# Splitting the output weights during the row maxima, and loading operands of pair 2 earlier, in a streaming encoder step

## The chip, the cores and the metric

The kernel runs on one core of a Trainium2 chip. The metric is the device time of one execution in microseconds (us); the figure of a kernel is the median of its runs. TensorE (PE) multiplies, with its weight loads shown as PEld; VectorE (DVE), ScalarE (ACT) and GpSimd (POOL) work on tiles in SBUF and PSUM; SyncE (SP) issues the transfers. Each engine takes its instructions in the order in which they were put into its queue, and waits on the first that is not ready.

## The reference

One layer of a streaming encoder is computed for a prompt of 2048 rows and a sample (decode) of 64 rows, with 1024 columns. One projection gives the input of an S5 branch, its gate, q, k, v, the gate of the attention, and forget logits. The attention has 8 heads of 64 columns, with a bias from the running sum of the forget logits:

```
logf = log_sigmoid(f_logit + b_f);  cum = cumsum(logf)
s = q k^T * scale + cum_q - cum_k, masked to pos_k <= pos_q
y_att = (softmax(s) v) * silu(z_a)
mixed = concatenate([y_ssm, y_att])            # (2048 + 64) x 1024
y = x + gate * (mixed @ w_out)                 # w_out is 1024 x 1024
```

The decode rows also attend to a cache of 512 rows. All data are float32; besides y, the kernel returns k, v, logf and the S5 states.

## The kernel before, in words

**Number format.** A float32 product is made as three products of two parts: `split` writes hi, rounded, on ACT (L319), and lo = x - hi on DVE (L323) or, where no engine is named, on POOL through `padd` (L205).

**Stages.** The input projection ends at about 620 us of the span, the S5 gate at about 800, attention (`Attn.run`) at about 1217, the output projection (`Out.run`) at 1391.

**Attention** goes over 20 tiles of a pair of heads and up to 512 query rows. A tile is done in units of two blocks of keys: TensorE makes scores into a `twin` of two PSUM banks, ACT exponentiates them into `p` (L354), DVE or POOL sums `p` into `acc` (L1489) for the denominators, and TensorE multiplies `p` with `vt` into `bank`. At a tile's end the sums are turned into a logarithm and an exponential `w` (two L354 on ACT), and `z`, the gated output, is multiplied on DVE (L1504) and POOL (L205) and stored in `ma_d` (L1519). Between the blocks the loop works ahead for later tiles: `step` loads k and q, `turn` transposes them on TensorE and splits them, and `maxima` makes each query row's largest score: TensorE computes the scores a first time and DVE adds the bias `cb` and takes the maximum (`pb`, `pm`, L1411). Three lists say what is still open: `todo` and `loaded` (k and q to be loaded, to be transposed), `mx` (maxima to be made), `smq` (maxima to be transposed into `sm`).

**Weights.** `Out.weights` is a generator which `Attn.run` advances twice per unit once all lists are empty. It loads the 16 blocks of w_out, 128 x 512 each, into a ring `ost` of three places (L1749, on SP), and two loads later splits a block: `ohb` on ACT, `olb` on POOL. Then it takes memory for the operands of the output, loads pair 0 of the S5 half (`load`, L1827), loads and splits the decode rows (L1909, L1910), and fetches the prepared operands t1 to t4 from DRAM (L1720). What is left of it `Out.run` finishes.

**Output.** The mixed rows are taken as pairs p = 0 to 7 of 128-row tiles. Pair 0 is multiplied plainly (`plain`: i the row tile, n the column half, j the half of the inner dimension; 0 is S5, 1 is attention). Pairs 1 to 7 use seven products instead of eight (`product`): sums and differences s1 to s4 of a pair's quarters a11, a12, a21, a22 are made by `differ` (1 and 3 on POOL, 2 and 4 on DVE: L1838, L1842) and split by ACT and DVE. The raw quarters come by `load(p)`: one 512 KB transfer from `ms_d` (tag m0) and one from `ma_d` (tag m1), each tag with one place. Evictions of PSUM into the `ot` ring of six are on DVE (L1878, L1881, L1882, L1816) and ACT (L1875); `residual` loads x (L1807), POOL adds (L205), SP stores the rows (L1821). `Out.run` is written as a fixed order: within it, each engine takes its instructions as the program has them, while in attention a scheduler places them.

Of the kernel before, what the change touches and what calls it, by code (L numbers as in the profile page):

```python
# [9 lines left out]
F32R = mybir.dt.float32r  # L10
# [7 lines left out]
P = 128  # L18
# [1164 lines left out]
class Attn:  # L1183
# [322 lines left out]
    def sums(self, tile):  # L1506
# [11 lines left out]
        e.pmul(tile.z, w[:, :n].rearrange("p (c t) -> p t c", t=TC), tile.z)  # L1518
        e.nc.sync.dma_start(e.ma_d[P * tile.hp:P * tile.hp + P, :, 64 * tile.qt:64 * tile.qt + n // TC], tile.z)  # L1519

    def run(self, out):

        e = self.e
# [2 lines left out]
            self.mem.ring(tag, int(1024 * kb), n)  # L1526
        self.hold("cb", 4, 3)
        weights = out.weights()
        pend = done = None
        self.forced = 0  # L1530
        self.vload(0)
        for i, (hp, qt) in enumerate(self.order):
# [15 lines left out]
            for u in range(0, len(blocks), PVG):  # L1548
                self.step()
                group = []  # L1550
                for kd, t in blocks[u:u + PVG]:
                    group.append(self.scores(tile, kd, t))
                    self.maxima()
                free = True
                if done and u:
                    self.sums(done)
                    done = None
                    free = False
                if pend:
                    self.mix(*pend)  # L1560
                    if pend[3]:
                        done = pend[0]
                pend = tile, group, u == 0, u + PVG >= len(blocks)
                if not u:
                    self.vload(i + 1)
                if free:
                    self.turn()
                if not (self.todo or self.loaded or self.mx or self.smq):
                    if not self.given:
                        out.mem.add(self.ring("kn"))  # L1570
                    out.mem.add(self.spare("cb", "ks", "qs", "sm"))
                    next(weights, None)
                    next(weights, None)
            if tile.acc[1] is not None and not tile.end:
# [2 lines left out]
        if done:  # L1577
            self.sums(done)

        out.mem.add(self.spare("vt"))  # L1580
        self.cur = self.seen = len(self.order)
        out.mem.add(self.spare("cb", "ks", "qs", "sm"))
        out.mem.join()
        for _ in range(16):
            if not out.cast:
# [82 lines left out]
class Out:  # L1668
# [12 lines left out]
    def __init__(self, e):  # L1681
        self.e = e
        self.mem = Region(e.nc)
        self.pre = Region(e.nc, R_PRE)
        self.b, self.a, self.x, self.acc, self.tmp, self.gate = {}, {}, {}, {}, {}, {}
        self.d, self.raw = [], []
        self.near = self.cast = False
        self.ops = {}

    def raw_operands(self, i):  # L1690
# [31 lines left out]
    def weights(self):  # L1722


        e = self.e
        mem = self.mem
        blocks = [(i, j) for i in range(2) for j in range(2)]

        def wait(n):
            while mem.room(2048) < n:  # L1730
                yield

        yield from wait(5)
        mem.ring("ost", 2048, 3)
        late = []

        def part():
            st, key = late.pop(0)
            h, l = (mem.tile([P, 512], F32R, name="o%s%s%d" % ((x,) + key)) for x in "hl")
            e.split(st, h, l, keep=True)  # L1740
            self.b[key] = h, l

        for k in range(4):
            for i, j in blocks:
                yield from wait(2)
                if len(late) == 2:
                    part()
                st = mem.tile([P, 512], F32, name="ost")
                e.nc.sync.dma_start(st, self.block(i, j, k))  # L1749
# [2 lines left out]
        while late:  # L1752
            yield from wait(2)
            part()
            yield
        for x in "hl":
            for name, n in (("a11", 1), ("a12", 1), ("a22", 2), ("s4", 1)):
                yield from wait(n)
                mem.ring("m" + x + name, 2048, n)
            mem.rings["m%sa21" % x] = mem.rings["m%ss4" % x]  # L1760
        while mem.room(4096) < 2:
            yield
        for j in range(2):
            mem.ring("m%d" % j, 4096, 1)
        self.load(0, 0)
        for j in range(2):
            yield from wait(2)
            mem.ring("ms%d" % (j + 1), 2048, 1)
# [1 line left out]
            self.decode_load(j)  # L1770
            yield
        yield
        for name in ("a11", "a21"):
            self.split(0, name, keep=True)
            yield
        for j in range(2):
            self.decode_split(j)
            yield
        self.cast = True
        for s in (1, 0):  # L1780
            for n in (1, 0):
                if s == n == 0:
# [152 lines left out]
    def run(self, weights):  # L1935

        e = self.e
        for tag, kb, n in (("x", 4, 1), ("ot", 2, 6), ("ms4", 2, 1), ("mhs2", 2, 1), ("mls2", 2, 1), ("mhs3", 2, 1),
                           ("mls3", 2, 1)):
            self.mem.ring(tag, 1024 * kb, n)  # L1940
        for i in range(2):
            m = self.a[0, "a%d2" % (i + 1)] = self.temp().rearrange("p (k c) -> p k c", k=4)
            e.nc.sync.dma_start(m, e.ma_d[:, 0, P * i:P * i + P].rearrange("(k p) c -> p k c", p=P))
        self.load(1, 1)
        for _ in weights:
            pass
        self.residual(2)
        self.decode(1)
        self.decode(0)

        self.fetch("t3", 3, [self.mem.at("late", x, [P, 512], F32R) for x in self.mem.rings["ost"][2][1:]])
        for i, n in ((0, 1), (1, 1), (0, 0), (1, 0)):
            self.plain(i, n, 0)
        for k in range(4):
# [2 lines left out]
        self.split(0, "a12", "a22")  # L1957
        self.differ(1, 1)
        self.differ(1, 3)
        self.differ(1, 2)  # L1960
        self.differ(1, 4)
        self.split(1, "a11", "s2")
        self.plain(0, 1, 1)
        self.plain(0, 0, 1)
        self.split(1, "s1", "a12")
        self.plain(1, 1, 1)
        self.split(1, "s3", "a22")
        self.load(2)
        self.plain(1, 0, 1)
        for p in range(1, 8):  # L1970
            q = p + 1 if p < 7 else 0
            self.split(p, "s4")
# [179 lines left out]
```

## Time and profile before

| | |
|---|---|
| runs | 1387.33, 1392.0, 1394.06 us, median 1392.0 |
| profiled execution | 1393.23 us, of which the span is 1391.4 us, mean granted clock 0.981 |
| PE, PEld busy | 1312.5 us (94%), 1031.9 us (74%) |
| DVE busy | 968.5 us (70%) |
| ACT busy | 652.0 us (47%) |
| POOL busy | 520.5 us (37%) |
| DMA | 204.92 MB, 147 GB/s on average |

The span runs from the first to the last instruction; 1.83 us of the execution lie around it. Busy shares are averages over stages with different limits: in the projections and the output TensorE is nearly always busy, so that any gap on it there is lost time, whereas other engines' gaps are not. A row of the timeline gives the start, the duration, the engine, the line, what is written and read, and in square brackets how long the engine had been idle before, and what ended that. A row of the waits gives the engine and line that waited, what it waited for, the total in us, how often, and the longest.

### The profile page before, as it was taken

To read this page: it belongs to the slowest core of one execution; us is meant where nothing else is said; L and a number is where in the kernel's file an instruction comes from. 1 tells how busy PE (TensorE), PEld (TensorE's weight loads), DVE (VectorE), ACT (ScalarE), POOL (GpSimd) and SP (SyncE) were. 2 spreads that over 40 slices of the span, in tenths; PEclk is the share of its full clock that TensorE was granted. 3 is DMA by queue.
4 is the path that set the end of the run, shared out by engine and by line. 5 is a ranking of instruction groups with operands and counts; after the bars stand their busy time and mean duration, and the time that the engine had idled before them with its cause. 6 is when DMAs were issued, how large, how long until landed. Compare 5 with 4: busy or idle time off the path is not lost.

```text
span 1391.4 us, 25886 instructions
## 1 busy us (share of the span) xinstructions
PE 1312.5 (94%) x9164; PEld 1031.9 (74%) x9164; DVE 968.5 (70%) x2404; ACT 652.0 (47%) x1710; POOL 520.5 (37%) x502
## 2 busy tenths in 40 slices
PE   5888999999999899999999899999999989898998
PEld 2886999998889899998879755555555554387887
DVE  3635896977877679864218877786787885446775
ACT  3645356567453576573315335445445445522211
POOL 1100254556534354452004113423423426743453
PEclk9899999999999999999999889999999999999999
DMA  9885333543546836446249624134121133495552
GB/s 342 318 309 124 100 86 94 154 123 107 163 133 217 282 110 180 145 141 196 84 138 291 202 73 121 32 91 125 43 70 48 40 65 79 146 330 169 182 164 78
DMA packets 249476, 204.92 MB, mean 147 GB/s; under 512 B 91296, under 2 KB 217340, under 8 KB 248322
## 3 DMA queue, kind: packets, MB, share of 16 engines
q1 hardware_dynamic: 249346, 203.27, 47.6%
q8 instruction: 72, 1.18, 0.4%
q14 instruction: 58, 0.48, 0.1%
HBM read 137.68 MB, written 65.53 MB: 146 GB/s over the span
## 4 chain that ended last, share of the span: by engine, by line
PE 63%; DVE 11%; DMA 6%; POOL 4%; issue 4%; ACT 3%; SPq 1%; DVEq 0%; ACTq 0%; POOLq 0%
PE low L154 25%; PE twin L154 13%; PE bank L154 12%; PE last L154 7%; PE glu L154 3%; DVE pb L1411 2%; PE bank L157 2%; DMA wst<-in_w_in_dram 1%; POOL qss L329 1%; POOL olb L205 1%; DMA lt<-t 1%; DVE acc L1489 1%; ACT p L354 1%; DVE ev L650 1%; DVE wlo L323 1%
## 5 line engine op out<-in xcount | busy, mean ns | idle before, releaser
L154 PE MATMUL low<-whi,h 128*128 128x256 f32 (+1 forms) x1584 | 296.3, 285 | 6.5 <-DVE th L609 3.5
L154 PE MATMUL low<-h,whi 128*128 128x256 f32 (+2 forms) x1152 | 277.6, 332 | 0.4 <-DVE h L323 0.3
L154 PEld LDWEIGHTS low<-whi,h 128*128 128x128 f32 x1584 | 247.9, 189 | 10.0 <-DVE th L609 3.7
L1411 DVE CUSTOM_DVE_ANT_0 pb<-twin,cb 128x512 bf16<-128x512 f32 (+3 forms) x328 | 199.9, 609 | 58.9 <-PE twin L154 49.1
L154 PE MATMUL low<-wlo,h 128*128 128x256 f32 (+1 forms) x816 | 229.1, 283 | 5.9 <-DVE wlo L323 5.9
L154 PEld LDWEIGHTS low<-h,whi 128*128 128x128 f32 x1152 | 195.5, 192 | 21.4 <-issue 2.8
L354 ACT ACTIVATE p<-twin 128x1024 f32<-128x1024 f32 (+3 forms) x180 | 149.7, 839 | 119.4 <-PE twin L154 107.2
L154 PE MATMUL low<-h,wlo 128*128 128x256 f32 (+2 forms) x576 | 188.2, 327 | 1.2 <-DVE wlo L323 1.2
L154 PEld LDWEIGHTS low<-wlo,h 128*128 128x128 f32 x816 | 154.3, 189 | 8.2 <-DVE wlo L323 7.7
L154 PE MATMUL bank<-p,vt 128*64 128x512 f32 (+3 forms) x704 | 142.5, 527 | 0.0
L154 PE MATMUL twin<-qs,ks 64*128 64x512 f32 (+3 forms) x1056 | 134.1, 359 | 0.0
L154 PEld LDWEIGHTS low<-h,wlo 128*128 128x128 f32 x576 | 110.3, 192 | 10.9 <-DVE wlo L323 2.6
L323 DVE TENSOR_TENSOR wlo<-wst,whi 128x512 fp32r<-128x512 f32 (+1 forms) x96 | 71.6, 752 | 59.9 <-ACT whi L319 59.7
L1489 DVE TENSOR_TENSOR acc<-acc,p 128x1024 f32<-128x1024 f32 (+4 forms) x88 | 90.2, 1025 | 30.5 <-ACT p L354 28.1
L329 POOL TENSOR_TENSOR qss<-qss,mhalf 128x4 f32<-128x4 f32 (+1 forms) x68 | 79.9, 1176 | 84.1 <-DVE qss L328 76.0
L154 PEld LDWEIGHTS twin<-qs,ks 64*128 64x128 f32 x1056 | 95.2, 191 | 11.0
L154 PE MATMUL twin<-sm,kb 64*128 64x512 f32 (+3 forms) x360 | 78.0, 428 | 21.2 <-DVE pm L1411 14.4
L319 ACT CAST whi<-wst 128x512 fp32r<-128x512 f32 (+1 forms) x96 | 58.7, 619 | 73.2 <-PE low L154 37.5
L154 PEld LDWEIGHTS bank<-p,vt 128*64 128x64 f32 x704 | 45.2, 140 | 63.8 <-issue 56.1
L205 POOL TENSOR_TENSOR x<-x,ot 128x512 f32<-128x512 f32 (+1 forms) x34 | 52.8, 1556 | 84.4 <-DVE ot L1816 79.7
L154 PEld LDWEIGHTS twin<-sm,kb 64*128 64x128 f32 x360 | 34.5, 187 | 61.8 <-DVE pm L1411 32.8
L646 ACT ACTIVATE hsq<-ev 128x64 bf16<-128x64 f32 (+1 forms) x272 | 69.7, 256 | 8.2
(437 smaller groups left out, 2634.2 us busy)
## 6 DMA issues: line engine op xcount, KB each, us to landing
wst<-in_w_in_dram SPq DMA_DIRECT2D x48, 512.0 KB
x<-in_x_prompt_dram SPq DMA_DIRECT2D x32, 512.0 KB
h<-h SPq DMA_DIRECT2D x16, 1024.0 KB
wada<-in_w_ada_dram SPq DMA_DIRECT2D x12, 1024.0 KB
cb<-cb_d SPq DMA_DIRECT2D x20, 512.0 KB
out_dram<-ev SPq DMA_DIRECT2D x64, 128.0 KB
out_dram<-x SPq DMA_DIRECT2D x32, 256.0 KB
z_d<-th SPq DMA_DIRECT2D x24, 256.0 KB
```

Source lines behind the costliest of these rows:

```text
L154: return self.keep(self.pe.matmul(*a, **kw))
L157: return self.keep(self.pe.transpose(*a, **kw))
L205: PL.tensor_tensor(out, x, y, op=op)
L319: i = S.copy(hi, x)
L323: V.tensor_tensor(lo, x, hi, op=ALU.subtract)
L329: PL.tensor_tensor(out, out, bc(mhalf[:out.shape[0]], list(out.shape)), op=ALU.pow)
L354: i = S.activation(out, x, func, **kw)
L646: S.activation(sq[:r], tv[:, h], AF.Square, accum_out=ss[:r, h:h + 1])
L650: V.tensor_tensor(tv, tv, e.bc(ss[:r].unsqueeze(2), [r, 4, HD]), op=ALU.mult)
L1411: V.tensor_tensor_reduce(b[:, :n], ps[:, h, :n], cb[:, h, :n], 1.0, NEG, ALU.add, ALU.max, accum_out=self.pm[:, t, h, pi:pi + 1])
L1489: (PL if j else V).tensor_tensor(y[:rows, :, c0:nq], x[:rows, :, c0:nq], p[:rows, :, :n], op=ALU.add)
```

## The change

The change does three things.

1. In `Attn.run` the generator is advanced as soon as `todo` and `loaded` are empty, that is while maxima (`mx`, `smq`) are still being made. A new function `give` hands the generator the memory that is free by then. The ring `ost` has four places instead of three, and the split follows three loads behind instead of two. `part` names DVE for the low half once no maxima are open; in the built program all 16 low halves are on POOL.
2. In `weights` the decode rows are loaded and split before pair 0's operands, and the splits of pair 0's a11 and a21 come after the point up to which attention advances the generator.
3. In `Out.run` the attention half of pair 0 and of pair 1 goes into `ot` places, m0 has two places, and pair 2's raw operands are therefore loaded right after the generator is finished, not four plain products later. The eviction of `plain(0, 1, 1)` comes before `differ(1, 2)` and `differ(1, 4)`, and splits of pair 1 come one plain product later.

The diff, cut to these:

```
+    def give(self, out):
+        if not self.given:
+            self.given.append(None)
+            out.mem.add(self.ring("kn"))
+            out.mem.add([(a / 1024, b / 1024) for a, b in self.mem.segs if b > a])
+            self.mem.segs = []
+        out.mem.add(self.spare("cb", "ks", "qs"))
+        if not (self.mx or self.smq):
+            out.mem.add(self.spare("sm"))
+        if len(self.values) == 24:
+            out.mem.add(self.spare("vt"))
...
-                if not (self.todo or self.loaded or self.mx or self.smq):
-                    if not self.given:
-                        out.mem.add(self.ring("kn"))
-                    out.mem.add(self.spare("cb", "ks", "qs", "sm"))
+                if not (self.todo or self.loaded):
+                    self.give(out)
                     next(weights, None)
                     next(weights, None)
...
-        yield from wait(5)
-        mem.ring("ost", 2048, 3)
+        yield from wait(6)
+        mem.ring("ost", 2048, 4)
...
-            e.split(st, h, l, keep=True)
+            e.split(st, h, l, el=e.V if self.idle() else None, keep=True)
...
-                if len(late) == 2:
+                if len(late) == 3:
                     part()
...
-        for i in range(2):
-            m = self.a[0, "a%d2" % (i + 1)] = self.temp().rearrange("p (k c) -> p k c", k=4)
-            e.nc.sync.dma_start(m, e.ma_d[:, 0, P * i:P * i + P].rearrange("(k p) c -> p k c", p=P))
-        self.load(1, 1)
+        for t in range(2):
+            for i in range(2):
+                m = self.a[t, "a%d2" % (i + 1)] = self.temp().rearrange("p (k c) -> p k c", k=4)
+                e.nc.sync.dma_start(m, e.ma_d[:, t, P * i:P * i + P].rearrange("(k p) c -> p k c", p=P))
         for _ in weights:
             pass
+        self.load(2)
...
+        self.plain(0, 1, 1)
         self.differ(1, 2)
         self.differ(1, 4)
-        self.split(1, "a11", "s2")
-        self.plain(0, 1, 1)
         self.plain(0, 0, 1)
-        self.split(1, "s1", "a12")
+        self.split(1, "a12", "a11")
         self.plain(1, 1, 1)
-        self.split(1, "s3", "a22")
-        self.load(2)
+        self.split(1, "a22", "s2")
         self.plain(1, 0, 1)
+        self.split(1, "s1", "s3")
```

Where the splits of w_out stand on ACT is seen in two pieces of its order. Before, from the last tile but its end, with `w` the closing steps of the tile before, `p` the exponentials and `ohb` the high half of a block of w_out:

```order
L354 ACTIVATE w_0_9212<-w_0_9212 128x512
L319 CAST ohb_166144_0_12657<-ost_2_12501 128x512
L319 CAST ohb_170240_0_12662<-ost_0_12469 128x512
L354 ACTIVATE p_0_9019<-twin_8167 128x1024
L354 ACTIVATE p_1_9033<-twin_9004 128x1024
L319 CAST ohb_83456_0_12691<-ost_1_12471 128x512
L319 CAST ohb_87552_0_12696<-ost_2_12501 128x512
L354 ACTIVATE p_2_9052<-twin_8163 128x1024
```

In the changed kernel the first of them, some 50 instructions earlier, at tiles whose followers' maxima are open (`sm` is such a transposed maximum):

```order
L319 CAST ohb_199808_0_12012<-ost_0_11966 128x512
L354 ACTIVATE p_3_9072<-twin_9004 128x2x128
L354 ACTIVATE p_4_9099<-twin_8167 128x2x128
L319 CAST ohb_9728_0_12056<-ost_1_11968 128x512
L319 CAST ohb_13824_0_12061<-ost_2_12010 128x512
L354 ACTIVATE p_5_9137<-twin_8163 128x2x128
L354 ACTIVATE p_0_9019<-twin_9004 128x2x128
L354 ACTIVATE w_0_9212<-bank_77 128x512
L354 ACTIVATE w_0_9212<-w_0_9212 128x512
L319 CAST ohb_17920_0_12110<-ost_3_12016 128x512
L319 CAST ohb_22016_0_12115<-ost_0_11966 128x512
L354 ACTIVATE p_1_9033<-twin_8167 64x2x128
```

All 16 casts moved ahead, two per unit as before, so that the exponentials of the last tile stand on ACT without a cast between them.

On SP, the loads of pair 2's raw operands (`m` from `ms_d` and `ma_d`) stood behind the late fetches and the first stores of the output. Before (t_68 and t_69 are t3 and t4 in DRAM, `x` is the residual):

```order
L1720 DMA lt_184576_0_12981<-t_68 128x512
L1807 DMA x_3_12984<-in_x_prompt_dram 128x1024
...
L1720 DMA ohb_95744_0_12730<-t_69 128x512
L1720 DMA olb_97792_0_12731<-t_69 128x512
L1807 DMA x_0_12890<-in_x_prompt_dram 128x1024
L1821 DMA out_dram<-x_1_12902 128x512 x2
L1821 DMA out_dram<-x_2_12904 128x512
L1827 DMA m_26112_0_12859<-ms_d 128x4x256
L1827 DMA m_30208_0_12942<-ma_d 128x4x256
```

In the changed kernel:

```order
L1733 DMA ht_188672_0_12984<-t_68 128x512
L1733 DMA lt_201856_0_12985<-t_68 128x512
L1841 DMA m_30208_0_12886<-ms_d 128x4x256
L1841 DMA m_62976_0_12989<-ma_d 128x4x256
L1821 DMA x_3_12991<-in_x_prompt_dram 128x1024
L1835 DMA out_dram<-x_0_12901 8x8x512 x2
L1733 DMA late_0_13037<-t_68 128x512
L1733 DMA late_1_13038<-t_68 128x512
```

The two loads moved up ahead of the decode rows' stores and of the ten late fetches, which stand behind them now. (Lines of the changed kernel are 13 to 15 higher.)

More of the change, by code (lines that the diff above doesn't have):

```diff
@@ L1528, in run @@
         weights = out.weights()
+        out.idle = lambda: not (self.mx or self.smq)
         pend = done = None
@@ L1578, in run @@
             self.sums(done)
-        out.mem.add(self.spare("vt"))
         self.cur = self.seen = len(self.order)
-        out.mem.add(self.spare("cb", "ks", "qs", "sm"))
+        self.give(out)
         out.mem.join()
@@ L1687, in __init__ @@
         self.near = self.cast = False
+        self.idle = lambda: False
         self.ops = {}
@@ L1755, in weights @@
             yield
[L1756 to L1765, printed above, removed]
         for j in range(2):
@@ L1772, in weights @@
         yield
-        for name in ("a11", "a21"):
-            self.split(0, name, keep=True)
-            yield
         for j in range(2):
@@ L1779, in weights @@
         self.cast = True
+        for x in "hl":
+            for name, n in (("a11", 1), ("a12", 1), ("a22", 2), ("s4", 1)):
+                yield from wait(n)
+                mem.ring("m" + x + name, 2048, n)
+            mem.rings["m%sa21" % x] = mem.rings["m%ss4" % x]
+        while mem.room(4096) < 3:
+            yield
+        for j in range(2):
+            mem.ring("m%d" % j, 4096, 2 - j)
+        self.load(0, 0)
+        yield
+        for name in ("a11", "a21"):
+            self.split(0, name, keep=True)
+            yield
         for s in (1, 0):
@@ L1949, in run @@
         self.decode(0)
-        self.fetch("t3", 3, [self.mem.at("late", x, [P, 512], F32R) for x in self.mem.rings["ost"][2][1:]])
+        self.fetch("t3", 3, [self.mem.at("late", x, [P, 512], F32R) for x in self.mem.rings["ost"][2][:2]])
         for i, n in ((0, 1), (1, 1), (0, 0), (1, 0)):
```

## The prediction

> **What bounds the kernel now.** I first read the windows of ten microseconds, to see where TensorE is not busy. Columns: stretch, its length, busy time (and instructions) of PE, PEld, DVE, ACT and POOL, granted clock, DMA share, GB/s.
>
> ```profile
> 1110.00:1120.00 10.00, 8.96 (x98) 5.28 (x94) 9.11 (x29) 3.03 (x7) 3.56 (x3) 1.00 0.01 2
> 1120.00:1130.00 10.00, 7.75 (x84) 4.74 (x80) 9.45 (x25) 3.88 (x7) 2.16 (x3) 1.00 0.52 91
> ...
> 1180.00:1190.00 10.00, 7.35 (x38) 3.39 (x36) 2.94 (x2) 6.94 (x10) 6.25 (x5) 0.83 0.47 134
> 1190.00:1200.00 10.00, 7.78 (x42) 3.02 (x38) 2.44 (x2) 3.46 (x5) 10.00 (x6) 0.89 0.58 176
> 1200.00:1210.00 10.00, 8.45 (x56) 4.22 (x56) 3.54 (x3) 6.45 (x9) 10.00 (x6) 0.93 0.32 101
> ...
> 1240.00:1250.00 10.00, 10.00 (x46) 8.27 (x45) 7.09 (x8) 2.18 (x4) 5.41 (x4) 1.00 1.05 399
> ...
> 1260.00:1270.00 10.00, 6.34 (x16) 4.87 (x16) 9.93 (x12) 3.46 (x7) 3.99 (x3) 0.66 0.16 64
> ```
>
> Three places stand out. In 1110 to 1130 VectorE is full (9.11 and 9.45 of 10) and TensorE waits a little: the row maxima are made there. In 1180 to 1210 neither PE, DVE nor ACT is full, and the granted clock falls to 0.83: something else ends the waits. In 1260 to 1270 PE has 6.34 of 10 and a clock of 0.66. Everywhere else that the change touches PE is the bound. So I asked the waits of 1160 to 1270 what ended them (total us, times, longest).
>
> ```profile
> ACT ohb L319 <- DMA ost<-in_w_out_dram: 18.7, 8, 4.7
> POOL ms L205 <- DMA m<-ma_d: 8.2, 1, 8.2
> DVE ms L1838 <- POOL ms L205: 8.0, 2, 5.5
> PE twin L154 <- ACT p L354: 6.4, 3, 2.6
> SPq L1749 <- POOL olb L205: 22.2, 10, 4.3
> ```
>
> Read from the bottom: SyncE cannot issue a load of w_out before POOL has made the low half of the block that holds the place (22.2 us); ACT's cast of the new block waits for that load (18.7 us); behind the cast, in ACT's order, stands the next exponential, and PE waits for that (6.4 us in 3 waits). The second chain is a transfer of pair 2's operands that POOL, then DVE, wait for.
>
> **Part 1: the splits of w_out leave the end of attention.** ACT's rows show the first chain, and PE's what it costs.
>
> ```profile
> 1182.95 0.62 ACT L319 CAST ohb<-ost 128x512 fp32r<-128x512 f32 x1 [3.83 <-DMA ost<-in_w_out_dram]
> 1194.67 0.62 ACT L319 CAST ohb<-ost 128x512 fp32r<-128x512 f32 x1 [4.75 <-DMA ost<-in_w_out_dram]
> ```
>
> ```profile
> 1180.70 0.50 PE L154 MATMUL twin<-sm,kb 64*128 64x512 f32 x2
> ...
> 1188.94 0.50 PE L154 MATMUL twin<-sm,kb 64*128 64x512 f32 x2
> ...
> 1190.98 1.94 PE L154 MATMUL bank<-p,vt 128*64 128x512 f32 x8
> 1192.85 0.50 PE L154 MATMUL twin<-sm,kb 64*128 64x512 f32 x2
> ...
> 1196.26 0.50 PE L154 MATMUL twin<-sm,kb 64*128 64x512 f32 x2 [2.22 <-ACT p L354]
> ...
> 1197.39 3.22 PE L154 MATMUL bank<-p,vt 128*64 128x512 f32 x8
> 1200.54 0.79 PE L154 MATMUL twin<-sm,kb 64*128 64x512 f32 x2
> ...
> 1204.80 0.50 PE L154 MATMUL twin<-sm,kb 64*128 64x512 f32 x2
> ...
> 1207.66 0.44 PE L154 MATMUL twin<-sm,kb 64*128 64x384 f32 x2 [1.55 <-ACT p L354]
> ```
>
> A unit of two score blocks and the product with v takes PE 1192.85 - 1188.94 = 3.91 us undisturbed. The unit from 1180.70 took 8.24, that from 1192.85 took 7.69, that from 1200.54 took 4.26: 4.33 + 3.78 + 0.35 over. With the wait of 1.55 at 1207.66 that is **10.0 us**. It holds the slow multiplies too: 3.22 instead of 1.94 for eight, behind a gap of 2.22 us. With the 16 casts gone from between these exponentials the units have no late load left, ACT has slack (6.94, 3.46, 6.45 of 10), and what is late next is PE itself. I take all 10.0; the least is the three bare waits, 6.4.
>
> **Part 2: where the splits go.** They go to about 1109 to 1152, two per unit, one unit being some 4 us. Three things cost there. ACT gets 16 x 0.62 = 9.9 us in 40, while it is busy 3.03 and 3.88 of 10: hidden, as long as the loads are there. POOL gets 16 low halves. DVE keeps its order, but it is the bound, and the rows below say what a busy POOL does to it. The first five are from 1165.6 to 1177.4, when POOL made six low halves without a pause; the last four are from 1110 to 1130 (the columns are busy us, mean ns | idle before).
>
> ```profile
> L205 POOL TENSOR_TENSOR olb<-ost,ohb 128x512 fp32r<-128x512 f32 x6 | 11.6, 1961 | 2.4 <-ACT ohb L319 2.3
> L1489 DVE TENSOR_TENSOR acc<-acc,p 128x768 f32<-128x768 f32 x1 | 1.8, 1848 | 0.1
> L1489 DVE TENSOR_TENSOR acc<-acc,p 128x512 f32<-128x512 f32 x1 | 1.6, 1598 | 0.1
> L1489 DVE TENSOR_TENSOR acc<-acc,p 128x256 f32<-128x256 f32 x1 | 1.3, 1317 | 0.1
> L1504 DVE TENSOR_TENSOR z<-bank,z 128x512 f32<-128x512 f32 x1 | 0.7, 678 | 0.0
> ```
>
> ```profile
> L1489 DVE TENSOR_TENSOR acc<-acc,p 128x512 f32<-128x512 f32 x2 | 1.4, 686 | 0.0
> L1489 DVE TENSOR_TENSOR acc<-acc,p 128x768 f32<-128x768 f32 x1 | 0.9, 948 | 0.0
> L1489 DVE TENSOR_TENSOR acc<-acc,p 128x256 f32<-128x256 f32 x2 | 0.8, 424 | 0.2 <-ACT p L354 0.2
> L1486 DVE COPY acc<-p 128x1024 f32<-128x1024 f32 x1 | 0.7, 687 | 0.0
> ```
>
> The same sums take 0.90, 0.91 and 0.89 us longer beside POOL, whatever their size; z<-bank, with one operand in PSUM, is not slowed (678 ns), so I take the maxima (pb<-twin,cb, also from PSUM) as not slowed. The five sums of the last rows, 5 x 0.90 = 4.5 us, lie in the stretch where DVE is full: all of it is on the path. The copy is bounded by 0 (like z) and 0.9 (like the sums); I take the middle, 0.5. From 1130 on DVE has room, and the same surcharge is covered.
>
> [...]
>
> The loads can be late here as they are at 1182.95. There are four places for raw blocks instead of three and the cast follows three loads behind, but POOL has its own sums to do beside 16 x 1.96 = 31 us of low halves in some 40 us, and the next load waits for it. Bounds: 0, and the 18.7 us of the waits above if nothing covers them. I take 1.0, near the lower end, since two blocks per 4 us need 3.9 us of POOL. Part 2 costs 4.5 + 0.5 + 1.0 = **6.0 us**.
>
> **Part 3: pair 2's operands.** The chain that ended last gives the rows (start, us, what), PE's timeline the last one.
>
> ```profile
> 1232.92 5.36 DMA lt<-t
> ...
> 1250.22 7.14 DMA m<-ma_d
> ...
> 1263.80 5.49 PE last L154 x12
> 1269.29 2.98 PE bank L154 x12
> ```
>
> ```profile
> 1263.80 0.79 PE L154 MATMUL last<-ohb,mha 128*128 128x512 f32 x1 [3.66 <-DVE ot L1882]
> ```
>
> The load was issued at 1250.22, behind the late fetches and the first stores of the output, and took 7.14 us in a busy stretch (399 GB/s). POOL's difference waited 8.2 us for it, DVE's L1838 5.5 us for POOL, and behind L1838 in DVE's order stand the evictions L1881 and L1882 for which PE waited 3.66 us. The twelve multiplies after the gap took 5.49 us, the next twelve 2.98: 2.5 more. In all **6.2 us**. Now the load stands directly behind the fetches of which the last landed at 1238.3; even issued only then and with the same 7.14 us it is there at 1245.4, before DVE comes to L1838 (5.5 before POOL's result at 1258.8, so 1253.3). What is late next is nothing that the rows show: PE goes on.
>
> What is moved past: the late fetches start behind 1 MB more, 2.6 us at 399 GB/s. Cost between 0 and 2.6; 0, because their stretch has no wait of PE before 1260. The moved evictions and splits (a plain product's eviction ahead of two differences, splits of pair 1 a product later) have the same instructions; a split that comes too late for product 6 of pair 1 could cost up to one such gap, 3.7 us, against a gain of at most nothing, since PE is full from 1220 to 1260 as the row of 1240 shows. I take 0. Pair 0's splits behind the last w cost ACT nothing on the path, since the decode rows' products come first.
>
> **The sum.** -10.0 - 6.2 + 6.0 = -10.2 against the profiled execution's own 1393.2 us: 1383.0. That execution lies 1.2 us above the median of the runs shown, so 1381.8 beside 1392.0. A measurement of this kernel tells about 0.5%, 7 us, from no change.
>
> **Rivals.** (a) The stretch of the maxima gives most of it back. For it: DVE is full there, and every microsecond shows. From 1108 to 1150 the waits are
>
> ```profile
> PE twin L154 <- DVE pm L1411: 3.8, 6, 1.3
> ```
>
> and the longest of 1.3 us, with two surcharges in one unit, comes to 3 us, more than the 2.22 that was followed by slow multiplies. With half of the 18.7 us of late loads added to 5.4: 14.8, net -1.4, 1390.6. Against it: the loads are spread over more time than in 1180 to 1210.
>
> [...]
>
> (b) The surcharge is covered: POOL's low halves fall between the sums. Then part 2 costs about 1, net -15.2: 1376.8. For it: the waits of PE in that stretch are short. Against it: POOL would be busy nearly throughout.
>
> (c) Another wait stands at the output, say the s2 split or a late fetch: part 3 is lost, net -4.0: 1388.0. The load's margin of 7.9 us speaks against it.
>
> (d) Slower: ACT's order couples late loads to the exponentials, now with no ACT or PE slack to cover them, while p's consumers on DVE are the bound. Then the whole 18.7 us is on the path, with 5.9 of the sums: 24.6, net +8.4, 1400.4. It decides against the change from a part 2 of 16.2 us on, and by over 0.5% from 23. For it: POOL is loaded to 31 us plus its sums; against it: four places, and DMA almost idle there (0.01 and 0.52).
>
> (e) The change does not do what it says: memory comes free so late that splits are still left at the end. The order has all of them ahead of the last tile, so only the timing could do it: about 1387.
>
> **How the numbers follow.** Forecast 0.48, (a) 0.20, (b) 0.14, (c) 0.07, (d) 0.07, (e) 0.04. Faster by over 0.5% (below 1385): nearly all of the forecast, (b), and a little of (a) and (e): 0.65. Slower by over 0.5% (above 1399): (d), 0.07. The rest, 0.28, is within. The range reaches from 1374 (b, with the 0.35 to 2 us by which part 1 can be larger) to 1394 ((a) with the full copy and a clock loss); outside lie (d) and the tails.
>
> **What would show it.** Right: no cast between exponentials after 1155 and the units of 1180 to 1205 at 3.9 us with a clock of 1.00; no PE gap at L1882 and L1838 without a wait for POOL; in 1110 to 1140 sums of 1.3 to 1.9 us on DVE, and PE's waits for DVE grown from 3.8 us to about 9. Wrong: ACT's casts waiting there for ost loads by more than 3 us in all, a granted clock below 1 in the stretch of the maxima, or a new gap at product 6 or 5 of pair 1.

## The result, and the profile after

The changed kernel takes 1379.56 us (median of 6 runs, 1376.9 to 1382.55) against 1392.57 for the kernel before (6 runs): a ratio of 0.9909, 95% interval 0.9883 to 0.9934, 13.0 us less. The forecast was 10.2 us less. The profiled execution took 1382.49 us with a span of 1380.5, which is 10.9 us less than the span of before.

TensorE's order is the same in both kernels, so that one and the same instruction can be looked up in both traces. Three of them cut the span into stages: the transposition of maxima at 1096.63, the product of `acc` with ones of the last tile but one, and that of the last tile. First the kernel before:

```profile
1096.63 0.48 PE L157 MATMUL bank<-identr,mq 128*73 128x128 f32 x4
...
1177.97 1.08 PE L154 MATMUL bank<-acc,ones 128*64 128x512 f32 x4
...
1215.38 1.08 PE L154 MATMUL bank<-acc,ones 128*64 128x512 f32 x4 [1.08 <-DVE acc L1489]
```

Then the changed kernel:

```profile
1097.49 0.48 PE L157 MATMUL bank<-identr,mq 128*73 128x128 f32 x4
...
1184.97 1.08 PE L154 MATMUL bank<-acc,ones 128*64 128x512 f32 x4
...
1210.95 1.03 PE L154 MATMUL bank<-acc,ones 128*64 128x512 f32 x4
```

The differences of these rows are the stages "maxima" (81.34 us before, 87.48 after), "last tile" (37.41, 25.98) and, up to the end of the span, "output" (176.02, 169.55). So 6.1 us were lost in the stretch of the maxima, 11.4 gained in the last tile, 6.5 gained in the output; 0.9 came in from earlier. The windows of ten microseconds show the same (length, PE, PEld, DVE, ACT, POOL, granted clock, DMA share, GB/s).

```profile
1110.00:1120.00 10.00, 8.26 (x85) 4.68 (x82) 9.58 (x23) 3.80 (x10) 6.88 (x5) 1.00 0.29 80
1120.00:1130.00 10.00, 7.46 (x88) 5.19 (x84) 8.39 (x24) 6.57 (x12) 8.89 (x7) 0.90 0.53 144
1130.00:1140.00 10.00, 9.75 (x64) 5.10 (x62) 6.70 (x19) 5.80 (x12) 6.43 (x6) 0.76 0.77 216
...
1150.00:1160.00 10.00, 9.01 (x68) 5.09 (x66) 7.26 (x22) 3.74 (x6) 2.48 (x2) 0.83 0.49 76
...
1180.00:1190.00 10.00, 10.00 (x72) 5.72 (x72) 1.92 (x2) 6.17 (x8) 3.81 (x2) 1.00 0.19 54
1190.00:1200.00 10.00, 10.00 (x60) 4.58 (x58) 3.80 (x3) 4.83 (x5) 6.34 (x4) 1.00 0.38 105
...
1250.00:1260.00 10.00, 10.00 (x45) 8.24 (x44) 8.39 (x11) 4.01 (x7) 3.13 (x2) 1.00 0.64 223
```

From 1180 on PE is full and the clock 1.00: the two holes of the kernel before are closed. In exchange POOL is busy 6.88 and 8.89 of 10 where it had 3.56 and 2.16, and the granted clock falls to 0.90 and 0.76 from 1120 to 1140, where it was 1.00 before. What ended the waits from 1100 to 1206:

```profile
PE twin L154 <- DVE pm L1411: 5.2, 6, 1.5
...
ACT ohb L319 <- DMA ost<-in_w_out_dram: 3.2, 2, 2.4
```

TensorE's waits for the maxima grew only from 3.8 to 5.2 us, so most of the 6.1 us is not in waits. Between the two landmarks of the stage TensorE runs the same 650 multiplies in both kernels. They keep it busy for 77.27 us at a granted clock of 1.00 before and for 81.37 us at 0.94 after, which is 4.1 us; its idle time, for whatever reason, grows from 4.07 to 6.11 us, which is 2.0. PE's timeline shows where the slow multiplies are:

```profile
1129.18 0.48 PE L154 MATMUL twin<-sm,kb 64*128 64x128 f32 x2 [1.53 <-DVE pm L1411]
...
1131.98 3.07 PE L154 MATMUL bank<-p,vt 128*64 128x512 f32 x8
...
1151.60 0.33 PE L154 MATMUL twin<-sm,kb 64*128 64x128 f32 x2 [0.99 <-DVE pm L1411]
...
1153.22 2.72 PE L154 MATMUL bank<-p,vt 128*64 128x512 f32 x8
```

Eight multiplies with v took 1.94 us where the granted clock was 1.00 (the eight at 1147.03). Behind these two waits they take 3.07 and 2.72, and the multiplies around them are slow as well: two dips of the clock, behind waits of 1.53 and 0.99 us.

### The profile page after: what moved, and what is told of

The parts are those of the page before. It is cut to its first block, busy times and chain, and to the rows that moved or that the text cites. A ratio compares the mean times of both kernels' runs of the same rounds, so it can differ in the third digit from the quotient of the medians.

```text
span 1380.5 us, 25881 instructions
## 1 busy us (share of the span) xinstructions
PE 1310.4 (95%) x9164; PEld 1030.5 (75%) x9164; DVE 970.6 (70%) x2404; ACT 652.6 (47%) x1710; POOL 513.8 (37%) x502
## 4 chain that ended last, share of the span: by engine, by line
PE 66%; DVE 12%; DMA 4%; issue 4%; POOL 3%; ACT 2%; SPq 0%; DVEq 0%; ACTq 0%; POOLq 0%
PE low L154 25%; PE twin L154 14%; PE bank L154 14%; PE last L154 7%; PE glu L154 3%; PE bank L157 2%; DVE pb L1411 2%; POOL qss L329 1%; DMA wst<-in_w_in_dram 1%; DVE wlo L323 1%; DMA z_d<-th 1%; POOL si L991 1%; DMA ht<-t 1%; POOL bb L205 1%; POOL si L1005 1%
## 5 line engine op out<-in xcount | busy, mean ns | idle before, releaser
L154 PEld LDWEIGHTS low<-h,whi 128*128 128x128 f32 x1152 | 194.4, 191 | 22.2 <-issue 2.8
L154 PEld LDWEIGHTS low<-h,wlo 128*128 128x128 f32 x576 | 109.9, 191 | 11.4 <-DVE wlo L323 3.0
L154 PEld LDWEIGHTS twin<-qs,ks 64*128 64x128 f32 x1056 | 95.2, 191 | 10.9
L1489 DVE TENSOR_TENSOR acc<-acc,p 128x1024 f32<-128x1024 f32 (+4 forms) x88 | 85.6, 972 | 24.4 <-ACT p L354 22.2
L154 PE MATMUL twin<-ks,qs 64*128 64x512 f32 (+3 forms) x328 | 71.9, 438 | 2.5 <-DVE pm L1411 1.5
```

The costliest lines, as they stand in the source:

```text
L154: return self.keep(self.pe.matmul(*a, **kw))
L1489: (PL if j else V).tensor_tensor(y[:rows, :, c0:nq], x[:rows, :, c0:nq], p[:rows, :, :n], op=ALU.add)
```

## The experiments

Theory: the last tile lost its time to ACT's casts, which waited for loads that waited for low halves on POOL; the output lost its own to the late load of pair 2; the changed kernel loses in the stretch of the maxima because POOL's low halves hold up DVE's sums. Rivals: the early splits bring nothing net and the output all; the loss in the maxima is ACT's or POOL's business, not DVE's; the order of evictions, not the load, matters in the output. The stages, from one profile each (start is the time of the first landmark), and the medians:

| run | start | maxima | last tile | output | median us | before, same chip |
|---|---|---|---|---|---|---|
| before | 1096.63 | 81.34 | 37.41 | 176.02 | 1392.57 | |
| changed | 1097.49 | 87.48 | 25.98 | 169.55 | 1379.56 | 1392.57 |
| e1_out_old | 1094.77 | 85.23 | 25.97 | 176.53 | 1385.56 | 1392.64 |
| e2_weights_old | 1095.88 | 84.15 | 27.44 | 170.33 | 1378.51 | 1392.64 |
| e4_evict_old | 1099.62 | 85.11 | 25.97 | 169.00 | 1378.0 | 1392.64 |
| e5_low_unread | 1096.59 | 80.78 | 25.97 | 169.66 | 1375.8 | 1392.64 |
| e7_start_later | 1097.30 | 83.10 | 25.97 | 169.63 | 1378.71 | 1393.43 |
| e8_weights_old_pool | 1096.49 | 80.94 | 33.80 | 169.87 | 1382.85 | 1393.43 |
| e9_low_unread_long | 1095.38 | 82.63 | 25.97 | 169.62 | 1375.32 | 1393.43 |
| e10_late_dve4 | 1095.28 | 80.98 | 26.56 | 169.98 | 1376.23 | 1393.43 |
| e11_load_alone | 1097.98 | 81.02 | 34.52 | 171.28 | 1384.66 | 1391.54 |
| e12_dve_alone | 1095.27 | 80.99 | 31.58 | 175.26 | 1388.22 | 1391.54 |
| e13_changed_again | 1098.37 | 86.51 | 25.97 | 169.65 | 1379.66 | 1391.54 |
| e14_late_dve4_again | 1093.92 | 81.00 | 26.54 | 169.94 | 1373.49 | 1391.54 |

The start differs by up to 5.7 us between profiles, for reasons that were not looked into; for one and the same kernel it differs by 0.9 us (changed) and 1.4 us (e10 and e14). That is why the stages are compared, and why a few us between two medians need many runs. A stage from one profile has a scatter of its own: the maxima took 87.48, 86.51, 85.23 and 85.11 us in the four runs that share the changed kernel's order there (changed, e13, e1, e4), the last tile 25.97 or 25.98 in all of them.

### The output: its order of before put back

```
         for _ in weights:
             pass
-        self.load(2)
...
-        self.plain(0, 1, 1)
         self.differ(1, 2)
         self.differ(1, 4)
+        self.split(1, "a11", "s2")
+        self.plain(0, 1, 1)
         self.plain(0, 0, 1)
-        self.split(1, "a12", "a11")
+        self.split(1, "s1", "a12")
         self.plain(1, 1, 1)
-        self.split(1, "a22", "s2")
+        self.split(1, "s3", "a22")
+        self.load(2)
         self.plain(1, 0, 1)
-        self.split(1, "s1", "s3")
```

> The changed kernel with the output's order of before: pair 2's raw operands are loaded after four plain products again, and evictions and splits of pair 1 stand as before; the early splits stay. Theory (the late load of pair 2 makes POOL, DVE and then TensorE wait, and the multiplies after the gap are slow): the gap of about 3.7 us at the eviction of product 7 of pair 1 comes back with some 2.5 us of slow multiplies, so 6 us more than the changed kernel, about 1386. Rival (the output gained through attention's end, where memory and transfers are free earlier): under 2 us more, about 1381.

Measured: 1385.56 us (ratio to before 0.9959, 0.994 to 0.9977), 6.0 more than the changed kernel, output 176.53. The chain that ended last, at that place, has the gap's follow-up, and PE's timeline the gap:

```profile
1254.28 0.70 DVE ot L1896
1254.97 0.04 issue
1255.02 5.49 PE last L154 x12
1260.51 2.99 PE bank L154 x12
```

```profile
1255.02 0.79 PE L154 MATMUL last<-ohb,mha 128*128 128x512 f32 x1 [4.44 <-DVE ot L1896]
```

It is the gap of the kernel before (3.66 there, 4.44 here), with the same slow twelve multiplies (5.49). The theory's 6 us are met.

### The output: only the order of evictions put back

The same edit, but `self.load(2)` stays early.

> The changed kernel with the order of evictions and splits in the output as before, but with the early load of pair 2. Theory (the load alone matters): the time of the changed kernel within 1.5 us, no gap at pair 2. Rival (evictions behind splits make TensorE wait): a gap of 2 to 4 us in the plain products or at pair 1, 3 to 6 us more.

Measured: 1378.0 us (0.9894, 0.9867 to 0.992), output 169.00, no gap of PE after 1160. The moved evictions and splits are worth nothing that can be seen; the load is.

### The output: the early load alone, on the kernel before

```
-        while mem.room(4096) < 2:
+        while mem.room(4096) < 3:
             yield
         for j in range(2):
-            mem.ring("m%d" % j, 4096, 1)
+            mem.ring("m%d" % j, 4096, 2 - j)
...
-        for i in range(2):
-            m = self.a[0, "a%d2" % (i + 1)] = self.temp().rearrange("p (k c) -> p k c", k=4)
-            e.nc.sync.dma_start(m, e.ma_d[:, 0, P * i:P * i + P].rearrange("(k p) c -> p k c", p=P))
-        self.load(1, 1)
+        for t in range(2):
+            for i in range(2):
+                m = self.a[t, "a%d2" % (i + 1)] = self.temp().rearrange("p (k c) -> p k c", k=4)
+                e.nc.sync.dma_start(m, e.ma_d[:, t, P * i:P * i + P].rearrange("(k p) c -> p k c", p=P))
         for _ in weights:
             pass
+        self.load(2)
...
         self.split(1, "s3", "a22")
-        self.load(2)
```

> The kernel before with the output's early load alone: the attention half of pair 1 in ot places, two places for m0, pair 2's operands loaded ahead of the decode rows. Splits of w_out and the order of evictions are as before. Theory: no gap at pair 2, the waits behind ACT's casts at attention's end stay, 6 us less than before, about 1386.5. Rival (the gap goes only together with the moved evictions, or another gap takes its place): less than 3 us gained.

Measured: 1384.66 us (0.9949, 0.993 to 0.9969), 6.9 less than before. The gap at pair 2 is gone; a new one of 1.67 us for a split of the decode rows (L1910) at 1219.0 explains why the output stage is 171.28 and not 169.6. By the stages only 4.7 of the gain is the output's, and 2.9 are in the last tile (34.52 instead of 37.41). The edit reaches that stage too: with its first line `weights` waits for room for three operands, and SyncE's order changes. Before, it issued four loads of the decode rows (L1902) with one of pair 0 (L1827) from 1172.62 to 1177.85, between loads of w_out. Here the four stand at 1121.6 to 1124.3, and the other four, of the attention half, at 1210.1, so late that the split waits for them: that is the new gap.

### The splits of w_out: at their old place, the engine as the program picks it

```
-                if not (self.todo or self.loaded):
+                if not (self.todo or self.loaded or self.mx or self.smq):
...
-        yield from wait(6)
-        mem.ring("ost", 2048, 4)
+        yield from wait(5)
+        mem.ring("ost", 2048, 3)
...
-                if len(late) == 3:
+                if len(late) == 2:
...
-        self.fetch("t3", 3, [self.mem.at("late", x, [P, 512], F32R) for x in self.mem.rings["ost"][2][:2]])
+        self.fetch("t3", 3, [self.mem.at("late", x, [P, 512], F32R) for x in self.mem.rings["ost"][2][1:]])
```

> The changed kernel with the splits of w_out where they were before (three raw places, advanced only when no maxima are open); the output stays as changed. Theory (the early splits gain 11 us at attention's end and cost 6.5 us in the stretch of the maxima): TensorE waits behind ACT's casts again at the end of attention, DVE's sums in the stretch of the maxima are undisturbed, in all 4.5 to 5 us more than the changed kernel, about 1384.5. Rival (the stretch of the maxima gives all of it back, and the whole gain is the output's): the same time as the changed kernel within 1.5 us.

Measured: 1378.51 us (0.99, 0.9871 to 0.9929). The theory said 1384.5, the rival the same time as the changed kernel: the rival's number came. But not by its mechanism: the last tile took 27.44 us, so that 10.0 of its 11.4 us of gain are there. The reason is a thing that the edit brought with it: with no maxima open, `idle` is true when the blocks are split, and all 16 low halves are on DVE. The run therefore says nothing on early or late alone, but it shows that most of the gain of the last tile can be had without early splits.

It shows a second thing. The maxima took 84.15 us, 2.8 more than before, although no low half runs there before 1168 and TensorE's waits for the maxima are those of before (3.8 us). The difference is slow multiplies behind a wait of 1.35 us that the kernel before has as well, at full clock: eight multiplies with v took 3.20 us behind it. A dip of the clock in this stretch therefore does not need the early splits.

### The splits at their old place, on POOL

The edit above, and `part` names no engine:

```
-            e.split(st, h, l, el=e.V if self.idle() else None, keep=True)
+            e.split(st, h, l, keep=True)
```

> The splits of w_out at their old place, with three raw places and, other than in the run in which DVE made them there, with all low halves on POOL as in the kernel before; the output as changed. Theory (at attention's end the slow low halves on POOL hold up the loads, the casts and so the exponentials): the gaps of 1.5 to 2.7 us behind late casts come back from 1180 to 1210, 10 us of loss there and none in the stretch of the maxima, about 1386, that is 6 us less than before and 6 more than the changed kernel. Rival (the place in time does not matter, early or late): within 1.5 us of the changed kernel.

Measured: 1382.85 us (0.9933, 0.9914 to 0.9952), 3.3 more than the changed kernel where 6 were expected. The waits from 1150 to 1212:

```profile
ACT ohb L319 <- DMA ost<-in_w_out_dram: 14.4, 7, 4.8
...
PE twin L154 <- ACT p L354: 5.4, 3, 2.5
```

The chain is back (18.7 and 6.4 us in the kernel before), and the maxima are free of loss (80.94). The last tile takes 33.80 us, 7.8 more than after the change: three quarters of the expected 10. The kernel before had 37.41. What this run does not share with it is the place of the decode rows' loads, which are not between those of w_out from 1164 to 1190; the run with the early load alone, where they had left this stretch too, had 34.52. So about 3 us of the last tile's gain go with these loads on SyncE. That is read from one profile of each; no run moves them alone.

### One word: the low halves on DVE, on the kernel before

```
-            e.split(st, h, l, keep=True)
+            e.split(st, h, l, el=e.V, keep=True)
```

> The kernel before with one word changed: the low halves of w_out are made by DVE, at their old place and with three raw places as before. Theory (POOL's slow low halves close the loop of load, cast and low half; early splits are not needed to break it): most of the 10 us at attention's end are gained, 7 to 10 us less than before, 1383 to 1386, with the gap at pair 2 still there. Rival (three places and loads issued too late are what hold up the casts): less than 4 us gained.

Measured: 1388.22 us (0.9979, 0.9964 to 0.9994), 3.3 less; last tile 31.58. By the time the rival's number came, by the stage something between (5.8 us of 11.4). The gap at pair 2 is still there (2.83 us). The waits from 1160 to 1216:

```profile
ACT ohb L319 <- DMA ost<-in_w_out_dram: 13.6, 7, 4.3
...
PE twin L154 <- ACT p L354: 3.1, 3, 1.9
```

So the slow low half (1.96 us on POOL in the mean of six before, 0.69 on DVE in the median of e2_weights_old) is one part of the chain; the theory gave POOL all of it, and that is too much. The three places are not the rest: with the same three places, the split two loads behind and DVE, but the changed kernel's output, the last tile took 27.44. What differs is SyncE's order. Here it issued a load of pair 0 and the four loads of the decode rows one behind the other from 1171.64 to 1177.54. The next load of w_out came at 1177.65, though DVE had freed its place with the low half that ended at 1172.92, and the cast that waited for this load waited 4.31 us, the longest. In the run with 27.44 no other load stands between those of w_out there, and no cast waited for over 2.9.

### The splits at their old place, four raw places, on DVE

```
-                if not (self.todo or self.loaded):
+                if not (self.todo or self.loaded or self.mx or self.smq):
```

> The splits of w_out at their old place, but with four raw places, a split three loads behind, and all low halves on DVE; the output as changed. Theory (the loop of load, cast and low half is what made casts late at attention's end; DVE takes half of POOL's time and is idle there, and the stretch of the maxima is left alone): no gap at attention's end over 1 us, none of the loss in the stretch of the maxima, so 1 to 3 us less than the changed kernel, 1377 or 1378. Rival (early splits are needed: the loads of w_out at the end are late whichever engine makes the low half): gaps of 2 us behind casts, 3 us or more above the changed kernel.

Measured: 1376.23 us (0.9879, 0.9858 to 0.9901), 3.3 less than the changed kernel, maxima 80.98, last tile 26.56, and ACT's casts wait 2.9 us in all for loads:

```profile
ACT ohb L319 <- DMA ost<-in_w_out_dram: 2.9, 2, 1.6
```

Run a second time beside the changed kernel on one chip:

> The changed kernel itself, beside the version with late splits on DVE on the same chip: 1378 to 1381, with a stretch of the maxima 3 to 7 us longer than that version's.

> The version with splits of w_out at their old place, four raw places and low halves on DVE, with the output as changed, beside the changed kernel on the same chip. Theory: 2 to 4 us less than the changed kernel, since it has the same gain at attention's end and none of the loss in the stretch of the maxima. Rival: within 1 us.

Measured: 1379.66 us (6 runs, 1375.74 to 1382.56) and 1373.49 us (4 runs, 1371.28 to 1374.57): 6.2 less, more than expected, with no overlap; maxima 86.51 and 81.00, last tile 25.97 and 26.54. The first runs of the same kernel lay higher (1374.27 to 1376.5), so that the gain over the changed kernel is 3 to 6 us. One condition more gives a kernel that beats both: 0.9867 of before (0.9845 to 0.9889).

### The maxima: low halves that read nothing

```
-            e.split(st, h, l, el=e.V if self.idle() else None, keep=True)
+            e.tc.keep_in_program_order(e.S.copy(h, st))
+            e.PL.memset(l.bitcast(F32), 0.0)
```

> The changed kernel in which POOL writes zeros into the low halves of w_out instead of reading the block and its high half and subtracting: the low halves of w_out are left out of the result. POOL has the same number of instructions there, but they read nothing from SBUF. Theory (DVE's sums with two SBUF operands are held up by POOL instructions that read SBUF): the sums of 256 to 1024 elements from 1110 to 1160 take their undisturbed 0.42 to 1.23 us, the waits of TensorE for DVE shrink, the granted clock stays at 1.00, 3 to 6 us less than the changed kernel. Rival (what is lost there is ACT's waits for loads and casts between exponentials): at most 1 us less.

Measured: 1375.8 us (0.9881, 0.986 to 0.9903), 3.8 less than the changed kernel; maxima 80.78, all of the loss gone, clock 1.00. But a write takes 0.525 us, a low half 1.28, so that POOL is also less busy. And the writes need no cast, so that most come earlier: six stand in 1108 to 1140, where the changed kernel has twelve low halves. Hence the same with three writes in place of one:

> The changed kernel in which POOL writes each low half three times with zeros, 3 x 0.525 us, so that it is busy there for longer than with the subtraction of 1.28 us, but reads nothing; the low halves of w_out are left out of the result. Theory (DVE's sums are held up by what POOL reads from SBUF): DVE's sums stay undisturbed and the time is that of the run with one write, 1375.8 within 1.5 us. Rival (POOL being busy is what costs: its own sums and products come late, or writes hold DVE up too): half or more of the difference to the changed kernel, 2 us or more, is lost again.

Measured: 1375.32 us (0.9872, 0.9851 to 0.9894), the time of the run with one write. POOL was not busy for longer here, as was meant: in 1108 to 1140 it has 18 writes and 16.8 us of work, in the changed kernel 22.2 us, since again most writes came earlier. So the time alone does not tell reading from being busy. Single instructions do. DVE's rows from 1108 to 1140, in the changed kernel:

```profile
L1489 DVE TENSOR_TENSOR acc<-acc,p 128x256 f32<-128x256 f32 x2 | 2.1, 1046 | 0.0
...
L1489 DVE TENSOR_TENSOR acc<-p,p 128x256 f32<-128x256 f32 x1 | 1.3, 1267 | 0.0
```

and with three writes that read nothing:

```profile
L1489 DVE TENSOR_TENSOR acc<-acc,p 128x256 f32<-128x256 f32 x2 | 0.8, 424 | 0.2 <-ACT p L354 0.2
L1489 DVE TENSOR_TENSOR acc<-p,p 128x256 f32<-128x256 f32 x1 | 0.4, 418 | 0.0
```

The sums of 256 elements go from 1.05 and 1.27 us to 0.42. Some of these sums ran beside writes: that at 1109.60, beside writes from 1107.95 to 1110.34, took 0.42. Two sums of 1024 elements, at 1077.04 and 1087.72, lay wholly within three writes each and took 1.23, as undisturbed; one at 1058.19 met a sum of POOL, which reads, and took 2.80. So in these profiles the sums were longer beside instructions of POOL that read, and not beside its writes. The stage still took 82.63 us, 1.3 more than before: the wait of 1.35 us was followed by slow multiplies here as well. In both runs the raw places also come free with ACT's cast instead of POOL's difference, so that loads come earlier too; PE waited for ACT 0.5 us there in the changed kernel, so this can be only a small part.

### The maxima: splits that start later

```
-                if not (self.todo or self.loaded):
+                if not (self.todo or self.loaded or len(self.mx) > 12):
```

> The changed kernel in which the generator is advanced only when at most twelve maxima are open: the splits start some 10 us later, eleven low halves on POOL and the last five, after the maxima, on DVE. Theory (each low half on POOL costs where it meets a sum on DVE while DVE is the bound): with fewer of them in the full stretch 1 to 3 us less than the changed kernel. Rival (the loss is the same wherever the sums are met, since a dip of the clock follows any of them): within 1 us of the changed kernel.

Measured: 1378.71 us (0.99, 0.9876 to 0.9924), between 1374.2 and 1382.82 in 6 runs: not to be told from the changed kernel by time. The first low half came 23 us later (1134.8 instead of 1111.3), not 10. By the stage it lost 83.10 - 81.34 = 1.8 us instead of 6.1, behind waits of 1.46 and 0.72 us at 1147.9 and 1152.7, and without any loss of clock (1.00 throughout). It fits the theory, but its spread leaves the verdict open.

## Why the prediction was right, point by point

**Part 1, the last tile: 10.0 us forecast, 11.4 measured.** The mechanism is as told: casts behind late loads ahead of exponentials. The 1.08 us at the last sums (before: `<-DVE acc`), which was left out of the sum, went as well. What the prediction did not see is that the early place is not needed for it: at the old place, with the decode rows' loads out of the stretch, low halves on DVE give 10.0 of the 11.4 with three raw places and 10.9 with four. Nor did it see that SyncE's loads of the decode rows have a part in the late casts (about 3 us, as read from the runs above). What was forecast came in the way that was forecast: the casts left, and no unit waits for one.

**Part 2, the maxima: 6.0 us forecast, 6.1 measured in the profile (5.2 in the second one, 3.9 and 3.8 in the two runs with an edited output), but made up otherwise.** The five sums were to pay 0.90 each, 4.5. The ones that paid are these, with the copy:

```profile
1111.72 1.14 DVE L1489 TENSOR_TENSOR acc<-acc,p 128x256 f32<-128x256 f32 x1
...
1117.51 1.27 DVE L1489 TENSOR_TENSOR acc<-p,p 128x256 f32<-128x256 f32 x1
...
1125.18 0.70 DVE L1486 COPY acc<-p 128x1024 f32<-128x1024 f32 x1 [0.38 <-ACT p L354]
...
1127.38 1.14 DVE L1489 TENSOR_TENSOR acc<-acc,p 128x768 f32<-128x768 f32 x1
...
1131.90 0.95 DVE L1489 TENSOR_TENSOR acc<-acc,p 128x256 f32<-128x256 f32 x1
...
1141.01 1.60 DVE L1489 TENSOR_TENSOR acc<-p,p 128x1024 f32<-128x1024 f32 x1
...
1146.57 2.15 DVE L1489 TENSOR_TENSOR acc<-acc,p 128x1024 f32<-128x1024 f32 x1
```

Up to 1132, against 0.42, 0.42, 0.95 and 0.42, that is 0.72 + 0.85 + 0.19 + 0.53 = 2.3 us, half of the forecast. POOL was not busy without a pause, and its low half took 1.28 us in the median, not 1.96. Only three of them are of the five: the two sums of 512 took 0.69 and paid nothing, and the sum p,p of 256 was not in the count. The copy, 0.5 in the sum, took its 0.70 and paid nothing. From 1130 on the surcharge was to be covered, and it was not: the two sums of 1024, 1.22 and 1.23 in the kernel before, pay 0.4 and 0.9 there, the wait for a maximum behind them grows from 0.56 to 0.43 + 0.99 us, and the second dip of the clock follows it.

The missing part is the clock, which the sum had at nothing and rival (a) had named: 3.07 - 1.94 and 2.72 - 1.94 are 1.9 us in two groups of multiplies, and 4.1 of the 6.1 us in the whole stage are slow multiplies. The price of the sums was too high, that of the clock missing, and the two errors offset each other: that part 2 came out at 6.1 is luck. How much clock is lost is in part chance too, since one dip came in the runs with 3.8 and 3.9 and two came in those with 6.1 and 5.2. The loads' 1.0 was near what PE saw of ACT's 3.2 us of waits, 0.27 and 0.23.

The signs that the prediction had set for itself say the same. Part 1's came: units of 3.9 us at a clock of 1.00 from 1187 on, and no cast between exponentials in the last tile (the last two stand at 1159.2). Of part 2's signs of being right, sums of 1.3 to 1.9 us and waits for DVE of about 9, neither came (0.95 to 1.27 for the slowed ones up to 1140, and 5.2). Two of its signs of being wrong came: ACT's casts waited more than 3 us for loads (3.2), and the granted clock fell below 1 in the stretch of the maxima (0.76).

**Part 3, the output: 6.2 us forecast, 6.5 measured.** Confirmed with its cause by putting load and evictions back (6.0 lost, and the evictions alone cost nothing) and by the load alone (4.7 gained in the output, with a new gap of 1.67; its other 2.9 of last tile belong to part 1). The moved evictions cost and brought nothing that can be seen, as taken.

**The rivals.** (a) came in half: the clock fell, the late loads came to 3.2 us and not to 9. (b) came for some of the sums only. (c): only a wait of 0.27 us was left. (d): ACT's waits for loads in the maxima were 3.2 us, not 18.7; its 5.9 us of sums are a slip, since the terms of (a) come to 5.4, and the transfers that it calls almost idle had a share of 0.52 in the second of its two windows. (e): no cast was left in the last tile, as the order said.

**The sum.** -10.2 against a span that is 10.9 less in the profile and 13.0 less in the median. The changed kernel's profiled execution is 2.9 us above its median, one of its two slowest, and that of before 0.7 above its own, so 2.3 of the 2.8 us between the forecast and the median are the choice of execution.

## What to carry to other kernels

When a cast waits for a load and the work behind it on its engine waits with it (before, the cast at 1194.67 had waited 4.75 us, the exponential behind it started at 1195.19, and TensorE waited for that from 1194.04 to 1196.26), look at the whole loop (places, depth, the engine that frees a place, what else stands in the queue of loads) before moving it in time: here a faster engine for the low half (0.69 us instead of 1.28 to 1.96), with the decode rows' loads out of the way, gave most of the gain at the old place (10.0 of 11.4 us), and one more place nearly all of it (10.9), without work on POOL in another stage. Before work is moved onto an engine that looks idle in a stretch, ask whether the engine that is the bound there is held up by what the other reads (here sums of 0.42 us took 1.05 and 1.27): the price is found where both already run side by side. And look at TensorE's clock behind short waits: here slow multiplies made 4.1 of the 6.1 us lost, and idle time 2.0. A load that a difference needs is issued ahead of stores and fetches that are needed later.

## What the runs showed of the hardware

**VectorE and GpSimd.** In the stretch of the maxima DVE sums of 256 elements with both operands in SBUF took 1.05 us in the mean of two, and 1.27, beside POOL instructions that read SBUF; beside POOL writes they took 0.42, as undisturbed, and sums of 1024 elements 1.23. Not every sum beside a reading POOL was longer: the one of 512 elements at 1130.75 took its 0.69 us, and the low half that POOL started at 1130.83 took 1.74, where the median is 1.28. With the copy it was the same: it started first and was not held up, POOL was:

```profile
1125.29 1.17 POOL L1588 TENSOR_TENSOR acc<-acc,acc 128x256 f32<-128x256 f32 x1
```

In the kernel before the same instruction took 0.73 us:

```profile
1121.53 0.73 POOL L1575 TENSOR_TENSOR acc<-acc,acc 128x256 f32<-128x256 f32 x1 [0.45 <-DVE acc L1489]
```

It is 0.44 longer; the copy, started 0.11 us earlier, still ran for 0.59. These are two instances in one profile. In the run with three writes the copy started 0.19 us after a write and took 0.88 instead of 0.69 us, 0.19 more, where the sums beside writes paid nothing; it is one instance:

```profile
L1486 DVE COPY acc<-p 128x1024 f32<-128x1024 f32 x1 | 0.9, 881 | 0.4 <-ACT p L354 0.4
```

**The clock.** In the stretch of the maxima multiplies became slow behind waits of 1.53 and 0.99 us. The wait of 1.53 was followed by slow multiplies in all four profiles of that order, the wait of 0.99 in two of them. A wait of 1.46 us in the run with later splits was followed by none. The wait of 1.35 us that the kernel before has there too,

```profile
1127.27 0.33 PE L154 MATMUL twin<-sm,kb 64*128 64x128 f32 x2 [1.35 <-DVE pm L1411]
```

was followed by slow multiplies in two of the ten profiles that have it: eight multiplies behind it took

```profile
1127.32 3.19 PE L154 MATMUL bank<-p,vt 128*64 128x512 f32 x8
```

in the run with three writes, and 1.67 at 1128.54 in the kernel before. So waits of 1.0 to 1.5 us, with shorter ones before them (0.29 to 0.73 us), were followed by slow multiplies in some executions and not in others. What decides it was not tried.
